# Encoder block on one core: head groups projected in order 0, 1, 2, the third rotated in a stack of its own, and its tiles stored by residue on the way out of PSUM

## The chip, the cores and the metric

The kernel runs on one core of a Trainium2 chip. The metric is the device time of one execution in microseconds (us). Five engines work side by side, each through its own queue in program order: TensorE (PE, matmuls; PEld is its weight load), VectorE (DVE), ScalarE (ACT), GpSimd (POOL) and SyncE (SP, which here issues most of the loads).

## The reference, cut to what matters

One layer over 512 positions of width 1024. Its attention branch has 12 heads of 128 dimensions in three groups of four, with dilations 1, 4 and 16, and a rotary turn of the first 32 dimensions of each query and key:

```python
q = partial_rope(q.reshape(B, S, n_heads, HEAD_DIM))
k = partial_rope(k.reshape(B, S, n_heads, HEAD_DIM))
for g, (window, dilation) in enumerate(ATTN_PATTERNS):        # (128,1), (512,4), (2048,16)
    sl = slice(g * HEADS_PER_GROUP, (g + 1) * HEADS_PER_GROUP)
    o_g, lse_g = dilated_window_attention(q[:, :, sl], k[:, :, sl], v[:, :, sl], dilation, window // (2 * dilation))
# partial_rope: concatenate([x1*cos - x2*sin, x2*cos + x1*sin, rest])
...
w_mix = jax.nn.softmax(jnp.stack(lses, axis=0), axis=0)
y_b = jnp.sum(w_mix[..., None] * o_all, axis=0).reshape(B, S, ATTN_GROUP_WIDTH)
```

Beside it stand a gated MLP branch (u, v through GELU, layer norm of v, a 128x128 spatial matmul), learned gates, an output projection and a feed-forward part of width 4096.

## The kernel before, in words

Everything is float32. A large matmul is done as three products of high and low parts (`mm3`, L84 to L86; a weight is split by ACT at L74 and DVE at L75, other tiles by ACT at L79 and DVE at L80). A projection of 128 features over 512 positions (`feature_tile`, PSUM tile `pf`) is 24 matmuls.

The attention stage runs over four values of `h`. `project_qk(h)` projects a query and a key tile for each of the three groups, six `pf` tiles in all, always with 128 features on the partitions and 512 positions along the row. Each tile is copied from PSUM by ACT twice: whole into `q1`, `k1` and so on (L331), and its first 32 rows into a stack `st` (L333), so that several tiles can be turned at once. `rotate` turns a stack: DVE swaps the halves of each 32 rows into `sw` (L311), POOL multiplies `sw` by the sine (L312), DVE multiplies `st` by the cosine (L313) and adds the two (L314), and ACT copies each 32 rows back into its tile (L316). Groups come in the order 1, 2, 0. Groups 1 and 2 share one stack (128 rows); group 0 has its own (64 rows).

Groups 1 and 2 work on positions by their residue modulo 4. The tiles keep natural order, and the score matmuls (`scores_b`, PSUM tile `psb`, L378, eight per value of `h`) pick every fourth column of query and key. Group 0 is split into high and low parts and scored in 128-position blocks (`scores_a`, tile `psa`). Each score tile goes through `softmax_tile` (DVE L364 and L366, ACT exponential L367). `mix(h)` weighs the groups: DVE prepares `xa`, PE multiplies it with a selection matrix (`pp`, L403), DVE and ACT work on four-column tiles up to `xc` (L405 to L424), PE does `pc` (L426), DVE gives `ca` (L430), and ACT scales the probabilities (L432, L434). `attend(h)` transposes the probabilities (`pt`, L453 and L466; split into `ptah`, `ptal`) and multiplies with the values (`py`, L483 to L490; L490 writes every fourth PSUM column). It runs within `project_qk(h + 1)`, and for the last `h` within the stage of the MLP branch.

After the attention loop comes the projection of v for the MLP branch (PSUM tile `pv`, 96 matmuls; GELU at L509 to L512, layer norm at L535 to L539 into `vln`), then four `pf` tiles for u, between which `pg` (L612) multiplies `vln` with the spatial weights. The weights of u are split by ACT (L74) and POOL (L75, input `uw`).

A scheduler puts the instructions of each engine's queue in an order when the kernel is built; the queues then run in that order and wait on semaphores. Pools give each named tile its buffers (`st` has two, `wpool` three weight tiles, PSUM tag `acc` four).

Of the kernel before, what the change touches and what calls it, by code (L numbers as in the profile page):

```python
# [10 lines left out]
F32 = mybir.dt.float32  # L11
F32R = mybir.dt.float32r
AF = mybir.ActivationFunctionType
ALU = mybir.AluOpType
PSUM = bass.MemoryType.PSUM

P = 128
S = 512
# [18 lines left out]
def block_kernel(ctx: ExitStack, tc: tile.TileContext, x, norm_mix_pre, w_in, b_gate, ln_v_gain, ln_v_bias,  # L37
                 w_spatial, b_spatial, w_branch_a, w_branch_b, w_out, norm_mix_post, norm_mlp_pre, w_up,
                 w_down, norm_mlp_post, ident_c, rope_c, mask_c, perm_c, out):
    nc = tc.nc  # L40
# [3 lines left out]
    def pool(stack, name, bufs=1, space=None, side=None):  # L44
        kw = {"side": side} if side else {}
        if space is not None:
            kw["space"] = space
        return stack.enter_context(tc.tile_pool(name=name, bufs=bufs, reuse_waits="tile", **kw))
# [14 lines left out]
    def wload(shape, srcs, name):  # L63
        raw = wpool.tile([P] + shape, F32, name=name, tag="raw")
        for dst, src in srcs(raw):
            nc.sync.dma_start(dst, src)
        return raw

    def wsplit(raw, pl=None, bufs=None, tag="w", sub=None):
        pl = pl or wpool  # L70
        shape = list(raw.shape)
        hi = pl.tile(shape, F32R, name="hi", tag=tag + "hi", bufs=bufs)
        lo = pl.tile(shape, F32R, name="lo", tag=tag + "lo", bufs=bufs)
        nc.scalar.activation(hi, raw, AF.Copy)  # L74
        (sub or nc.vector).tensor_tensor(lo, raw, hi.bitcast(F32), op=ALU.subtract)  # L75
        return hi, lo

    def split_into(hi, lo, src):
        nc.scalar.activation(hi, src, AF.Copy)  # L79
        return nc.vector.tensor_tensor(lo, src, hi.bitcast(F32), op=ALU.subtract)  # L80
# [199 lines left out]
    def feature_tile(wh, wl, nk, mh, ml, tag="acc"):  # L280
        ps = psA.tile([P, S], F32, name="pf", tag=tag, bufs={"acc": 4, "S": 2, "T": 1, "y": 1}[tag])
        for k in range(nk):
            mm3(ps, (wh[:, k], wl[:, k]), (mh[:, k], ml[:, k]), k == 0, k == nk - 1)
        return ps

    def fcols(wap, c0, nk, n, raw=None):
        return wap[:, c0:c0 + n].rearrange("(k p) c -> p k c", p=P)
# [3 lines left out]
    rows = gmlp.tile([32, P], F32, name="rows")  # L291
    wsp = gmlp.tile([P, 4, P], F32, name="wsp")
    proj = ExitStack()
    apool = pool(proj, "apool")
    rope = apool.tile([P, 2, S], F32, name="rope")
# [9 lines left out]
    by_r = perm[:, 2 * P:2 * P + 4].unsqueeze(1).unsqueeze(1)  # L305
    by_c = perm[:, 2 * P + 4:2 * P + 8].unsqueeze(1).unsqueeze(3)

    def rotate(st, tiles):
        rows = 32 * len(tiles)
        sw = apool.tile([P, S], F32, name="sw")  # L310
        nc.vector.stream_shuffle(sw[:rows], st[:rows], [(i + 16) % 32 for i in range(32)])  # L311
        nc.gpsimd.tensor_tensor(sw[:rows], sw[:rows], rope[:rows, 1], op=ALU.mult)  # L312
        nc.vector.tensor_tensor(st[:rows], st[:rows], rope[:rows, 0], op=ALU.mult)  # L313
        nc.vector.tensor_tensor(st[:rows], st[:rows], sw[:rows], op=ALU.add)  # L314
        for i, d in enumerate(tiles):
            nc.scalar.activation(d[0:32], st[32 * i:32 * i + 32], AF.Copy)  # L316

    def project_qk(h):
        got, tiles = {}, []
        for g in (1, 2, 0):  # L320
            if g == 2 and h:
                attend(h - 1)
            if g != 2:
                st, tiles = apool.tile([P, S], F32, name="st", bufs=2), []
            hd0 = (g * NH + h) * HD
            raw = wload([2, KD, P], lambda r: [(r[:, 0], fcols(w_in, COL_Q + hd0, KD, P)), (r[:, 1], fcols(w_in, COL_K + hd0, KD, P))], "qkw")
            for j, nm in enumerate("qk"):
                wh, wl = wsplit(raw[:, j])
                ps = feature_tile(wh, wl, KD, nhn, nln)
                d = apool.tile([P, S], F32, name=f"{nm}{g}")  # L330
                nc.scalar.activation(d, ps, AF.Copy)  # L331
                i = len(tiles)
                nc.scalar.activation(st[32 * i:32 * i + 32], ps[0:32], AF.Copy)  # L333
                tiles.append(d)
                got[nm, g] = d.rearrange("p (l r) -> p r l", r=4)
            if g == 2:
                rotate(st, tiles)
                scores_b(h, got)
            elif g == 0:
                rotate(st, tiles)  # L340
        for nm, t in zip("qk", tiles):
            w = S if nm == "q" else S + P
            o = 0 if nm == "q" else ROT
            hi = apool.tile([P, w], F32R, name=f"{nm}0h")
            lo = apool.tile([P, w], F32R, name=f"{nm}0l")
            split_into(hi[:, o:o + S], lo[:, o:o + S], t)
            if nm == "k":
                for z, y in ((hi, nc.scalar), (lo, nc.vector)):
                    zf = z.bitcast(F32)
                    for dst, src in ((z[:, 0:ROT], zf[:, S:S + ROT]), (z[:, S + ROT:], zf[:, ROT:2 * ROT])):  # L350
                        if y is nc.scalar:
                            y.activation(dst, src, AF.Copy)
                        else:
                            y.tensor_copy(dst, src)
            got[nm, 0] = (hi, lo)
        scores_a(h, got)

    stat = {}
    probs = {}
# [10 lines left out]
    def scores_b(h, got):  # L370
        md = small.tile([P, 2, 4], F32, name="mdb", bufs=2)
        stat[h, "md", "b"], stat[h, "m", "b"], stat[h, "d", "b"] = md, md[:, 0], md[:, 1]
        for r2 in range(2):
            ps = psA.tile([P, 2, 2, P], F32, name="psb", tag="S", bufs=2)
            for rr in range(2):
                r = 2 * r2 + rr
                for g in (1, 2):
                    nc.tensor.matmul(ps[:, rr, g - 1], got["q", g][:, r], got["k", g][:, r], start=True, stop=True)  # L378
            for rr in range(2):
                softmax_tile(h, "b", 2 * r2 + rr, ps[:, rr], masks[:, 4:6])  # L380

    def scores_a(h, got):
        md = small.tile([P, 2, 4], F32, name="mda", bufs=2)
        stat[h, "md", "a"], stat[h, "m", "a"], stat[h, "d", "a"] = md, md[:, 0], md[:, 1]
        (qh, ql), (kh, kl) = got["q", 0], got["k", 0]
        for c2 in range(2):
            ps = psA.tile([P, 2, 2, P], F32, name="psa", tag="S", bufs=2)
            for cc in range(2):
                c = 2 * c2 + cc
                qs, ks = slice(c * P, (c + 1) * P), slice(c * P, c * P + 2 * P)  # L390
                mm3(ps[:, cc], (qh[:, qs], ql[:, qs]), (kh[:, ks], kl[:, ks]), True, True)
            for cc in range(2):
                c = 2 * c2 + cc
                m = (masks[:, 0:3:2], masks[:, 1:3], masks[:, 1:3], masks[:, 1:4:2])[c]
                softmax_tile(h, "a", c, ps[:, cc], m)
# [40 lines left out]
    def attend(h):  # L436
        for _ in attend_steps(h):
            pass
# [55 lines left out]
    for h in range(NH):  # L494
        project_qk(h)
        mix(h)
# [96 lines left out]
    for g2 in range(2):  # L593
        raw = wload([KD, 2 * P], lambda r: [(r, fcols(w_in, COL_U + g2 * 2 * P, KD, 2 * P))], "uw")
        for j in range(2):
            g = 2 * g2 + j
            wh, wl = wsplit(raw[:, :, j * P:(j + 1) * P], sub=nc.gpsimd)
            ps = psA.tile([P, S], F32, name="pf", tag="acc" if g else "T", bufs=4 if g else 1)
# [87 lines left out]
    for d in range(GSTD):  # L686
        g2 = gate_rows(d - GSTD)
        raw = gate_raw(d)
        for br in range(2):
            ps = feature_tile(*wsplit(raw[:, :, 1 - br]), KD, nhn, nln)  # L690
# [85 lines left out]
    for t in range(4):  # L776
# [18 lines left out]
        r = rstd_of(ss, 1.0 / D)  # L795
# [187 lines left out]
def _constants():  # L983
    half = 16
    inv = (np.float32(500000.0) ** (-np.arange(0, 32, 2, dtype=np.float32) / np.float32(32))).astype(np.float32)
    ang = np.arange(S, dtype=np.float32)[:, None] * inv[None, :]
    cos, sin = np.cos(ang).astype(np.float32).T, np.sin(ang).astype(np.float32).T
    rope = np.tile(np.stack([np.concatenate([cos, cos]), np.concatenate([-sin, sin])]).astype(np.float32), (1, 4, 1))
    i = np.arange(P)[:, None]
    j = np.arange(P)[None, :]  # L990
    lo = i <= j
    hi = j <= i
    valid = [lo & (j >= ROT), lo, hi, hi & (j < ROT), np.abs(i - j) <= 64, (i - j) % 4 == 0]
    masks = np.stack([np.where(v, np.float32(0), np.float32(NEG)) for v in valid]).astype(np.float32)
    sel = (j // 4 == i % 32).astype(np.float32)
    by = [(np.arange(P)[:, None] % 4 == np.arange(4)[None, :]), (np.arange(P)[:, None] // 32 == np.arange(4)[None, :])]
    perm = np.concatenate([sel.T, sel] + [b.astype(np.float32) for b in by], axis=1).astype(np.float32)
    return {"ident_c": np.eye(P, dtype=np.float32), "rope_c": rope, "mask_c": masks, "perm_c": perm}
# [17 lines left out]
```

## Time and profile before

| what | value |
|---|---|
| median of 3 runs | 835.42 us (835.19 to 835.52) |
| the profiled execution | 831.64 us |
| its span, first to last instruction | 829.9 us |
| PE busy | 812.1 us (98%) |
| DVE, ACT, POOL busy | 489.7, 411.0, 58.0 us |
| mean granted TensorE clock | 0.995 |

A busy PE is a PE with a matmul in flight; it does not say at what pace. So beside the waits of PE one reads the distance between matmuls of a kind and the granted clock. Idle time of another engine matters only where PE waits for it.

### The profile page before, as it was taken

What the parts mean: (1) busy time and instruction counts of PE and PEld (TensorE: products, weight loads), DVE (VectorE), ACT (ScalarE), POOL (GpSimd) and SP (SyncE); (2) the same over time, 40 slices, a digit from 0 to 9 for tenths busy, and PEclk for the clock granted to TensorE, in tenths of its full rate; (3) what the DMA queues carried; (4) which work ended last, traced back from release to release, by engine and by line L of the source; (5) the groups of instructions that cost most, each with busy time, mean ns of one, the idle gap of its engine ahead of it and who ended that gap; (6) DMA issues with size and microseconds to landing.
All of it is one profiled execution on the core that took longest, in us unless ns stands there. A gap on an engine that the chain in (4) does not pass through costs nothing.

```text
span 829.9 us, 11578 instructions
## 1 busy us (share of the span) xinstructions
PE 812.1 (98%) x4629; PEld 721.4 (87%) x4629; DVE 489.7 (59%) x819; ACT 411.0 (50%) x689; POOL 58.0 (7%) x77
## 2 busy tenths in 40 slices
PE   9999999999999699999999999999999999999996
PEld 6899888888888488999998899999999888888885
DVE  6762245535353687787856559989888543333324
ACT  6342365857564535444535456666567533223311
POOL 3011010101012310000001210000000000000000
PEclk9999999999999899999999999999999999999999
DMA  9277323131312254342457221334333643222202
GB/s 311 98 256 209 86 72 102 51 102 51 102 52 57 58 199 127 94 115 77 129 177 226 104 102 52 112 117 129 103 102 103 228 152 102 90 82 87 98 1 102
DMA packets 84056, 95.73 MB, mean 115 GB/s; under 512 B 2417, under 2 KB 70033, under 8 KB 82978
## 3 DMA queue, kind: packets, MB, share of 16 engines
q1 hardware_dynamic: 80208, 77.60, 30.7%
q0 software_dynamic: 3792, 17.39, 6.1%
q8 instruction: 36, 0.59, 0.3%
q14 instruction: 18, 0.15, 0.1%
q10 hardware_dynamic: 2, 0.00, 0.0%
HBM read 86.60 MB, written 8.39 MB: 114 GB/s over the span
## 4 chain that ended last, share of the span: by engine, by line
PE 93%; DVE 4%; DMA 2%; ACT 1%; issue 0%; SPq 0%; DVEq 0%; POOLq 0%; ACTq 0%
PE pacc L885 11%; PE pd L84 9%; PE pd L86 9%; PE pd L85 9%; PE pf L84 8%; PE pf L85 8%; PE pf L86 8%; PE pgacc L560 6%; PE ptp L885 4%; PE pv L85 3%; PE pv L86 3%; PE pv L84 3%; PE pgS L560 2%; PE psb L378 2%; DMA w0raw<-in_w_in_dram 1%; PE py L490 1%
## 5 line engine op out<-in xcount | busy, mean ns | idle before, releaser
L84 PE MATMUL pf<-nh,hi 128*128 128x512 f32 x240 | 95.7, 399 | 0.3 <-DVE xd L428 0.3
L85 PE MATMUL pf<-nl,hi 128*128 128x512 f32 x240 | 95.2, 397 | 0.0
L86 PE MATMUL pf<-nh,lo 128*128 128x512 f32 x240 | 95.1, 396 | 0.0
L85 PE MATMUL pd<-hl,hh 128*128 128x512 f32 x224 | 87.2, 389 | 0.0
L84 PE MATMUL pd<-hl,hh 128*128 128x512 f32 x224 | 86.2, 389 | 0.0
L86 PE MATMUL pd<-hl 128*128 128x512 f32 x224 | 86.0, 389 | 0.0
L885 PE MATMUL pacc<-nt,hl 128*128 128x256 f32 x504 | 67.6, 280 | 0.1
L80 DVE TENSOR_TENSOR hl<-hid,hh 128x512 fp32r<-128x512 f32 x28 | 19.2, 692 | 75.6 <-ACT hh L79 75.6
L885 PEld LDWEIGHTS pacc<-nt,hl 128*128 128x128 f32 x504 | 62.6, 188 | 0.5 <-ACT hl L79 0.3
L75 DVE TENSOR_TENSOR lo<-qkw,hi 128x1024 fp32r<-128x1024 f32 x24 | 29.4, 1226 | 55.4 <-ACT hi L74 53.9
L79 ACT ACTIVATE hh<-hid 128x512 fp32r<-128x512 f32 x28 | 17.4, 630 | 89.0 <-PE pd L85 89.0
L84 PEld LDWEIGHTS pf<-nh,hi 128*128 128x128 f32 x240 | 45.7, 190 | 9.6 <-DVE xd L428 0.4
L86 PEld LDWEIGHTS pf<-nh,lo 128*128 128x128 f32 x240 | 45.6, 190 | 9.0
L85 PEld LDWEIGHTS pf<-nl,hi 128*128 128x128 f32 x240 | 45.6, 190 | 8.8
L86 PEld LDWEIGHTS pd<-hl 128*128 128x128 f32 x224 | 42.0, 188 | 8.8
L85 PEld LDWEIGHTS pd<-hl,hh 128*128 128x128 f32 x224 | 42.0, 188 | 8.8
L84 PEld LDWEIGHTS pd<-hl,hh 128*128 128x128 f32 x224 | 42.0, 188 | 8.5
L80 DVE TENSOR_TENSOR hl<-dnw,hl 128x1024 fp32r<-128x1024 f32 x32 | 39.1, 1225 | 13.9 <-ACT hl L79 13.9
L885 PE MATMUL pacc<-n,hl 128*128 128x256 f32 x336 | 45.2, 279 | 0.4 <-ACT z L910 0.4
L79 ACT ACTIVATE hl<-s 128x1024 fp32r<-128x1024 f32 x28 | 29.6, 1058 | 29.1 <-DVE s L869 10.8
L885 PEld LDWEIGHTS pacc<-n,hl 128*128 128x128 f32 x336 | 41.9, 188 | 0.6 <-ACT z L910 0.6
L74 ACT ACTIVATE hi<-qkw 128x1024 fp32r<-128x1024 f32 x24 | 25.4, 1058 | 32.1 <-PE pf L85 24.4
(315 smaller groups left out, 1966.9 us busy)
## 6 DMA issues: line engine op xcount, KB each, us to landing
upw<-in_w_up_dram SPq DMA_DIRECT2D x16, 1024.0 KB, 5.5
dnw<-in_w_down_dram SPq DMA_DIRECT2D x16, 1024.0 KB, 4.9
qkw<-in_w_in_dram SPq DMA_DIRECT2D x24, 512.0 KB, 5.4
gw<-in_w_in_dram SPq DMA_DIRECT2D x16, 512.0 KB, 5.1
slab<-in_w_in_dram SPq DMA_DIRECT2D x6, 1024.0 KB, 9.3
sum<-sum POOLq DMA_DIRECT2D x4, 1024.0 KB, 7.9
nt<-sum POOLq DMA_DIRECT2D x4, 1024.0 KB, 6.3
wow<-in_w_out_dram SPq DMA_DIRECT2D x4, 1024.0 KB, 4.9
```

The costliest lines, as they stand in the source:

```text
L74: nc.scalar.activation(hi, raw, AF.Copy)
L75: (sub or nc.vector).tensor_tensor(lo, raw, hi.bitcast(F32), op=ALU.subtract)
L79: nc.scalar.activation(hi, src, AF.Copy)
L80: return nc.vector.tensor_tensor(lo, src, hi.bitcast(F32), op=ALU.subtract)
L84: nc.tensor.matmul(ps, ah, bh, start=start, stop=False)
L85: nc.tensor.matmul(ps, ah, bl, start=False, stop=False)
L86: return nc.tensor.matmul(ps, al, bh, start=False, stop=stop)
L378: nc.tensor.matmul(ps[:, rr, g - 1], got["q", g][:, r], got["k", g][:, r], start=True, stop=True)
L490: nc.tensor.matmul(o, v12[:, g, r, hs], ptb[r // 2][:, r % 2, g], start=False, stop=(r == 3 and g == 1), skip_group_check=True)
L560: nc.tensor.matmul(ps, a[:, j], b[:, j], start=first and not (j or i), stop=(j == KH - 1 and i == 2), skip_group_check=True)
L885: nc.tensor.matmul(ps, a[:, j], b[:, j], start=first and not (j or m), stop=(j == KH - 1 and m == 2), skip_group_check=True)
```

## The change: what it does

The groups are projected in the order 0, 1, 2. Groups 0 and 1 share the stack of 128 rows; group 2 gets rows 64 to 127 of another. `scores_a` follows the first rotation, `scores_b` comes last. For groups 1 and 2 the two copies from PSUM read every fourth column, so that the tiles lie in SBUF by residue, and the score matmuls read 128 columns in a row. The rotary table has natural order for its first 64 rows and residue order for the other 64. The product with the sine is done by DVE.

```diff
-    def rotate(st, tiles):
-        rows = 32 * len(tiles)
+    def rotate(st, tiles, r0):
+        rows = slice(r0, r0 + 32 * len(tiles))
         sw = apool.tile([P, S], F32, name="sw")
-        nc.vector.stream_shuffle(sw[:rows], st[:rows], [(i + 16) % 32 for i in range(32)])
-        nc.gpsimd.tensor_tensor(sw[:rows], sw[:rows], rope[:rows, 1], op=ALU.mult)
-        nc.vector.tensor_tensor(st[:rows], st[:rows], rope[:rows, 0], op=ALU.mult)
-        nc.vector.tensor_tensor(st[:rows], st[:rows], sw[:rows], op=ALU.add)
+        nc.vector.stream_shuffle(sw[rows], st[rows], [(i + 16) % 32 for i in range(32)])
+        nc.vector.tensor_tensor(st[rows], st[rows], rope[rows, 0], op=ALU.mult)
+        nc.vector.tensor_tensor(sw[rows], sw[rows], rope[rows, 1], op=ALU.mult)
+        nc.vector.tensor_tensor(st[rows], st[rows], sw[rows], op=ALU.add)
         for i, d in enumerate(tiles):
-            nc.scalar.activation(d[0:32], st[32 * i:32 * i + 32], AF.Copy)
+            nc.scalar.activation(d[0:32], st[r0 + 32 * i:r0 + 32 * i + 32], AF.Copy)
     def project_qk(h):
-        got, tiles = {}, []
-        for g in (1, 2, 0):
-            if g == 2 and h:
-                attend(h - 1)
-            if g != 2:
-                st, tiles = apool.tile([P, S], F32, name="st", bufs=2), []
+        got, tiles, r0 = {}, [], 0
+        st = apool.tile([P, S], F32, name="st", bufs=2)
+        for g in range(3):
+            if g == 2:
+                st, tiles, r0 = apool.tile([P, S], F32, name="st", bufs=2), [], 64
+                if h:
+                    attend(h - 1)
...
-                nc.scalar.activation(d, ps, AF.Copy)
-                i = len(tiles)
-                nc.scalar.activation(st[32 * i:32 * i + 32], ps[0:32], AF.Copy)
+                view = ps.rearrange("p (l r) -> p r l", r=4) if g else ps
+                i = r0 + 32 * len(tiles)
+                for dst, src in ((st[i:i + 32], view[0:32]), (d, view)):
+                    nc.scalar.activation(dst.rearrange("p (r l) -> p r l", r=4) if g else dst, src, AF.Copy)
                 tiles.append(d)
-                got[nm, g] = d.rearrange("p (l r) -> p r l", r=4)
-            if g == 2:
-                rotate(st, tiles)
-                scores_b(h, got)
-            elif g == 0:
-                rotate(st, tiles)
+                got[nm, g] = d.rearrange("p (r l) -> p r l", r=4)
+            if g:
+                rotate(st, tiles, r0)
+            if g == 1:
+                scores_a(h, split_qk(tiles[:2]))
+        scores_b(h, got)
+
+    def split_qk(tiles):        # the split of q0, k0 that stood at the end of project_qk
...
-    rope = np.tile(np.stack([np.concatenate([cos, cos]), np.concatenate([-sin, sin])]).astype(np.float32), (1, 4, 1))
+    rope = np.stack([np.concatenate([cos, cos]), np.concatenate([-sin, sin])]).astype(np.float32)
+    by_residue = rope.reshape(2, 32, S // 4, 4).transpose(0, 1, 3, 2).reshape(2, 32, S)
+    rope = np.concatenate([rope, rope, by_residue, by_residue], axis=1)
```

The queues change as follows at three places. Lines of the changed kernel are up to seven higher (L378 becomes L383, L426 becomes L431, L539 becomes L544).

First, PE at the end of the attention loop, behind the last products of the values with the probabilities of h = 2 (`py`). Before:

```order
L86 MATMUL pv<-hi,nl 128x512
L490 MATMUL py<-ptb,v_89 128x128 x4
L403 MATMUL pp<-xa,perm 128x32
L426 MATMUL pc<-xc,perm 128x16
L84 MATMUL pf<-nh,hi 128x512
```

PE in the changed kernel at the same place:

```order
L85 MATMUL pv<-lo,nh 128x512
L495 MATMUL py<-ptb,v_89 128x128 x4
L408 MATMUL pp<-xa,perm 128x32
L86 MATMUL pv<-hi,nl 128x512
...
L86 MATMUL pv<-hi,nl 128x512
L431 MATMUL pc<-xc,perm 128x16
L84 MATMUL pv<-hi,nh 128x512
```

All 96 `pv` matmuls stood ahead of `pp` and `pc` before; now 34 of them stand between the two and 27 behind `pc`. For h = 1 and h = 2 the distance from `pp` to `pc` grows from 34 `pf` matmuls to 43.

Second, DVE at the last rotation of h = 3. Before, that of group 0, with its split behind it:

```order
L311 STREAM_SHUFFLE sw<-st 64x512
L313 TENSOR_TENSOR st<-st,rope 64x512
L314 TENSOR_TENSOR st<-st,sw 64x512
L80 TENSOR_TENSOR ptal<-pt,ptah 128x512
L80 TENSOR_TENSOR q0l<-q_2067,q0h 128x512
L80 TENSOR_TENSOR k0l<-k_2099,k0h 128x512
```

DVE in the changed kernel at the last rotation of h = 3, that of group 2:

```order
L311 STREAM_SHUFFLE sw<-st 64x512
L312 TENSOR_TENSOR st<-st,rope 64x512
L313 TENSOR_TENSOR sw<-sw,rope 64x512
L369 ISA p,mda<-psa,masks 128x256
L369 ISA mda 128x1
L369 ISA p,mda<-psa,masks 128x256
L369 ISA mda 128x1
L314 TENSOR_TENSOR st<-st,sw 64x512
```

The sum of the rotation now stands behind two softmax steps of group 0, which wait for `psa` on PE. On PE, 14 projection matmuls, `psa`, four transposes, six `py` and 15 projection matmuls stand between the end of the last key tile and the first `psb`.

Third, DVE in the layer norm of v, behind the end of the `pv` matmuls. Before:

```order
L519 COPY cols<-ptr 128x32
L539 TENSOR_SCALAR vln<-vln,mv,rs_out 128x512
L512 SCALAR_TENSOR_TENSOR vln<-gt,pv 128x512
L80 TENSOR_TENSOR ptal<-pt,ptah 128x512
L512 SCALAR_TENSOR_TENSOR vln<-gt,pv 128x512
L535 BN_STATS st_2360<-vln 128x6
L80 TENSOR_TENSOR ptal<-pt,ptah 128x512
```

DVE in the changed kernel at the same place:

```order
L542 BN_AGGR mv<-st_2332 128x2
L80 TENSOR_TENSOR ptal<-pt,ptah 128x512
L540 BN_STATS st_2346<-vln 128x6
L90 TENSOR_SCALAR rs_in<-mv 128x1
L80 TENSOR_TENSOR ptal<-pt,ptah 128x512
L515 SCALAR_TENSOR_TENSOR gt<-gt,pv 128x512 x2
L542 BN_AGGR mv<-st_2346 128x2
L544 TENSOR_SCALAR vln<-vln,mv,rs_out 128x512
```

The two `ptal` of the last `attend` moved ahead of the first `vln` normalization. On PE the first two `pg` of u's first tile follow the last `attend`'s first products, the third stands 18 `pf` and eight `py` matmuls further on. Behind the start of the gates only a few neighbours on PE change places, and SP issues the same loads in the same sequence throughout.

More of the change, by code (lines that the diff above doesn't have):

```diff
@@ L330, in project_qk @@
                 d = apool.tile([P, S], F32, name=f"{nm}{g}")
-                nc.scalar.activation(d, ps, AF.Copy)
-                i = len(tiles)
-                nc.scalar.activation(st[32 * i:32 * i + 32], ps[0:32], AF.Copy)
+                view = ps.rearrange("p (l r) -> p r l", r=4) if g else ps
+                i = r0 + 32 * len(tiles)
+                for dst, src in ((st[i:i + 32], view[0:32]), (d, view)):
+                    nc.scalar.activation(dst.rearrange("p (r l) -> p r l", r=4) if g else dst, src, AF.Copy)
                 tiles.append(d)
-                got[nm, g] = d.rearrange("p (l r) -> p r l", r=4)
-            if g == 2:
-                rotate(st, tiles)
-                scores_b(h, got)
-            elif g == 0:
-                rotate(st, tiles)
+                got[nm, g] = d.rearrange("p (r l) -> p r l", r=4)
[5 more added lines that the diff above has]
+    def split_qk(tiles):
+        got = {}
         for nm, t in zip("qk", tiles):
@@ L355, in project_qk @@
             got[nm, 0] = (hi, lo)
-        scores_a(h, got)
+        return got
     stat = {}
```

## The prediction

> **What bounds the kernel now.** I read the page first (busy time, the chain that ended last), then the waits of PE alone, then the attention stage by groups, the chain in order of time, and the clock around the longest wait.
>
> ```profile
> PE 812.1 (98%) x4629; PEld 721.4 (87%) x4629; DVE 489.7 (59%) x819; ACT 411.0 (50%) x689; POOL 58.0 (7%) x77
> PE 93%; DVE 4%; DMA 2%; ACT 1%; issue 0%; SPq 0%; DVEq 0%; POOLq 0%; ACTq 0%
> PE pc L426 <- DVE xc L424: 4.7, 1, 4.7
> PE pt L466 <- DVE ptal L80: 2.6, 1, 2.6
> PE pf L84 <- DVE xd L428: 0.3, 1, 0.3
> PE py L483 <- ACT ptah L79: 0.3, 1, 0.3
> ```
>
> PE is the bound: 93% of the chain lies on it. So only two things can move the time: fewer or faster matmuls, and the waits of PE. The waits are few, and the largest stand where the attention loop ends. The last four rows are PE's waits: total, times, longest.
>
> Next, the pace of the score matmuls, beside matmuls of the same 128x128 shape whose operands lie in a row:
>
> ```profile
> L378 PE MATMUL psb<-k,q 128*128 128x128 f32 x64 | 16.7, 416 | 0.0
> L490 PE MATMUL py<-ptb,v 128*128 128x128 f32 x64 | 8.6, 275 | 0.0
> L378 PEld LDWEIGHTS psb<-k,q 128*128 128x128 f32 x64 | 15.7, 326 | 0.2
> L490 PEld LDWEIGHTS py<-ptb,v 128*128 128x128 f32 x64 | 8.1, 191 | 0.2
> ...
> 114.24 0.93 PE psb L378 x4
> 115.41 2.79 PE psb L378 x12
> 118.43 0.23 PE pf L85
> 153.05 3.73 PE psb L378 x16
> 181.53 0.89 PE py L490 x8
> 195.41 0.93 PE psb L378 x4
> 196.57 0.92 PE psb L378 x4
> 238.77 0.93 PE psb L378 x4
> 239.93 0.92 PE psb L378 x4
> ```
>
> The last rows are the chain: start, length, what. Each `psb` takes 0.233 us of PE (3.73/16), each `py` 0.111 (0.89/8), each `pf` or `pv` 0.23.
>
> **The change, part by part.**
>
> *Scores from tiles stored by residue (gain 7.8).* Both operands of `psb` are now read with a step of four columns; afterwards both lie in a row, as those of `py` do. Their number stays: 64 in the trace. 64 x (0.233 - 0.111) = 7.8 us, all on PE and so on the path. Ends: 0, if the step does not set the pace, and 7.8; I take 7.8, because the weight load too is 326 ns against 191 for the same shape.
>
> *Copies out of PSUM with a step (ACT; 0 on the path).*
>
> ```profile
> L331 ACT ACTIVATE k<-pf 128x512 f32<-128x512 f32 x11 | 6.4, 581 | 0.1
> L316 ACT ACTIVATE k<-st 32x512 f32<-32x512 f32 x12 | 7.6, 630 | 0.3
> 95.00:130.00 35.00, 35.00 (x155) 29.66 (x154) 13.45 (x30) 18.95 (x35) 3.44 (x2) 1.00 0.30 83
> 170.00:200.00 30.00, 30.00 (x156) 26.22 (x155) 11.97 (x43) 16.79 (x35) 1.73 (x1) 1.00 0.27 80
> 230.00:260.00 30.00, 30.00 (x151) 25.91 (x151) 16.56 (x55) 19.92 (x43) 5.88 (x3) 1.00 0.24 71
> ```
>
> (The windows give PE, PEld, DVE, ACT, POOL busy time, then the clock.) Eight copies per h take the step. No row has ACT reading PSUM that way. The floor is no extra; the nearest row is the stepped weight load, 326 - 191 = 135 ns more for 128 columns, so 0.54 us for 512. Eight of them are 4.3 us per h; ACT is busy some 60% of these windows, so it keeps about 16 us free in the 41 us of one h. I take the upper end, 0.54, and cost it at nothing on the path where the next part shows cover for it. The Trainium skill ("Advanced Engine Details and Errata", PSUM Cachelines) says that any non-contiguous access to PSUM significantly slows matmuls. Row L490 disagrees for writes: it writes every fourth column and keeps 0.111. Reads by ACT no run here shows; by the rule they would be dearer, which is the first rival below.
>
> *The last rotation of each h (group 2, 64 rows; 0).*
>
> ```profile
> L311 DVE STREAM_SHUFFLE sw<-st 64x512 f32<-64x512 f32 x4 | 2.9, 731 | 0.0
> L313 DVE TENSOR_TENSOR st<-st,rope 64x512 f32<-64x512 f32 x4 | 2.7, 681 | 0.1
> L312 POOL TENSOR_TENSOR sw<-sw,rope 64x512 f32<-64x512 f32 x4 | 7.0, 1752 | 53.3 <-DVE sw L311 29.2 <-DVE nm L366 24.1
> L364 DVE CUSTOM_DVE_ANT_0 p<-psa,masks 128x256 f32<-128x256 f32 x8 | 3.1, 418 | 0.0
> ```
>
> The sine product costs DVE eight more products of 0.68 (5.5 us in all) instead of 1.75 each on POOL; a rotation alone is no longer for it (0.73 + 3 x 0.68 = 2.8 us). Behind the end of the last key tile PE has 14 `pf` (3.2), `psa` (12 at about 0.12, 1.4), four transposes and six `py` (1.2) and 15 `pf` (3.4): `psb` is due after 9.2 us. The chain: the sum of the rotation queues behind two softmax steps, and these wait for half of `psa` (3.2 + 0.7), 0.4 each: 4.7; sum 0.7: 5.4; the `ptb` copy and two copies of 0.63 on ACT: 7.2. Two us are spare. The stepped copies delay the start of the rotation by 0.54, which hides, since the sum waits for `psa` anyway. Without this cover each h would pay what exceeds 2 us. The 128-row rotation has 62 `pf` (14 us) between its last tile and `psa`. POOL loses 14 us of work which nobody on the path waited for.
>
> *The wait of `pc` (gain 6.9).*
>
> ```profile
> 272.71 2.04 DVE L409 TENSOR_TENSOR big<-mab,mdb 128x4 f32<-128x4 f32 x1
> 276.64 0.17 DVE L424 TENSOR_TENSOR xc<-cf,perm 128x16 f32<-128x16 f32 x1
> 277.00:280.00 3.00, 2.73 (x7) 2.19 (x8) 1.41 (x4) 3.00 (x8) 0.00 (x0) 0.50 0.08 25
> 278.34 0.63 PE L85 MATMUL pf<-nl,hi 128*128 128x512 f32 x1
> 278.76 0.63 PE L86 MATMUL pf<-nh,lo 128*128 128x512 f32 x1
> 281.32 0.58 PE L86 MATMUL pf<-nh,lo 128*128 128x512 f32 x1
> 272.39 2.34 POOL L75 TENSOR_TENSOR lo<-uw,hi 128x1024 fp32r<-128x1024 f32 x1 [4.47 <-ACT hi L74]
> ```
>
> PE waits 4.7 us for the DVE chain, then 0.3, and then runs at a granted clock of 0.50: eight `pf` stand 0.42 apart (278.34 to 278.76) in place of 0.23, 1.5 us, and `pc` itself some 0.4. Sum 6.9. Afterwards 34 `pv` (7.8 us) lie between `pp` and `pc`. From `pp` to `xc` DVE took under 5 us, 2 of them beside a POOL product. But now group 2's scores come last, so the chain also runs from `psb`: the queue puts the exponentials of group 0, a weight split on ACT and DVE, two pairs of softmax steps and four exponentials ahead, which I add up to about 9 us; `pc` is due 12 us after `psb` starts. Spare about 3, and one POOL product of 2.3 can eat most of it. So gain 6.9 at best, 0 if all the slack is misjudged; I take 6.9. Next late is what follows `pv`.
>
> *The layer norm of v (gain 3.0, loss 3.5).*
>
> ```profile
> 278.93 1.28 DVE L510 SCALAR_TENSOR_TENSOR gt<-gt,pv 128x512 f32<-128x512 f32 x2 [1.04 <-ACT gt L509]
> 286.55 2.46 DVE L539 TENSOR_SCALAR vln<-vln,mv,rs_out 128x512 f32<-128x512 f32 x1
> 298.77 0.55 DVE L539 TENSOR_SCALAR vln<-vln,mv,rs_out 128x512 f32<-128x512 f32 x1 [0.44 <-POOL rs_out L96]
> ```
>
> The 2.6 and 0.3 us that PE waits for `ptal` and `ptah` should go, as the two `ptal` now precede the slow normalization: 2.9, say 3.0. But in the kernel before, the stretch from the first GELU product to the last `vln` lasts 298.77 + 0.55 - 278.93 = 20.4 us, and it began 8 us after the last `pv`, because `pc` held it. Now it begins at once, while PE gets to the `pg` that needs the last `vln` after 8 transposes, 24 `pf`, about 4 us of small matmuls, 21 `pf` and eight `py`: 0.9 + 5.5 + 4 + 4.8 + 0.9 = 16.1 us. DVE needs 20.4, less a 0.7 product that moved behind, less up to 1.9 by which the 2.46 exceeds its 0.55 sister. So PE waits 1.7 to 4.9 here, in several pieces. I take 3.5.
>
> *The rest (0).* The loads keep their sequence and sizes on SP; weights of a tile are split two tiles ahead.
>
> Sum: 7.8 + 6.9 + 3.0 - 3.5 = 14.2 us. The profiled execution would go from 831.64 to 817.4. It stands 3.8 us below the median of the runs shown; carried over in us, 835.42 - 14.2 = 821.2.
>
> **The rivals.**
>
> 1. *The stepped copies make ACT the bound (slower).* If ACT's read of PSUM costs far more than the weight load suggests, the eight copies fill ACT. Its 16 us free per h are used up at 2.0 us extra per copy; beyond that each h grows by eight times the rest. At 16/8 + 14.2/32 = 2.4 us extra (3.0 in place of 0.58) the gain is gone; at 3 us extra it is 4 x 8 = 32 us lost, 853. The Trainium skill's rule ("Advanced Engine Details and Errata", PSUM Cachelines), taken at its worst, leads here; it gives no size. For it: no row shows such a read. Against it: the step costs PE a factor of two, not five.
>
> 2. *The wait of `pc` stays.* The exponentials of both groups, the weight split and a POOL product then end after the 34 `pv`. The stall, once some 4 us long, brings the half clock with it: the 6.9 are not gained, 828. For it: 3 us of slack against one 2.3 us POOL product. Against it: the three inner h have 43 matmuls there and no POOL product.
>
> 3. *The MLP part takes more.* If DVE's burst is held by POOL's splits of u again, and the half clock follows the wait, the loss is 4.9 + 1.9 rather than 3.5: 824.5.
>
> 4. *The step does not set the pace of `psb`.* Then the 7.8 fall away: 829. Against it stand both rows of L378.
>
> **How the numbers follow.** Forecast as summed, 817 to 823.5: 0.60. Rival 3, to 827: 0.17. Rival 2: 0.09. Rival 4: 0.04. More than I count, under 817: 0.03. A mixture of losses that ends within 0.2%: 0.02. Rival 1: 0.05. The likeliest gives 821.2; the range 816 to 827 takes in rival 3 and the bounds of the layer norm, and leaves out rivals 1, 2 and 4 and the mixture, 0.20 together. So faster by over 0.2% 0.93, within 0.2% (1.7 us, about what a measurement can tell from no change) 0.02, slower 0.05.
>
> **What would show it.** `psb` matmuls 0.11 us apart and weight loads near 190 ns; no wait of PE for `xc`, and no granted clock near 0.5 beside it; waits of PE for `vln` or for ACT ahead of `pg`, 2 to 5 us together; stepped copies between 0.58 and 1.1 us; no POOL product in the attention stage. The prediction is wrong if PE waits in the attention loop itself, for `q2` or `k2`, or if `psb` keeps its pace.

## The result: 20 us faster, and the profile after

The changed kernel takes 815.28 us (814.79 to 815.90, 4 runs) beside 835.31 us (834.69 to 835.52): ratio 0.976, interval 0.9745 to 0.9779. The direction was forecast; the time lies 5.9 us below the 821.2 and 0.7 us below the range. Its four runs stand in two pairs, at 814.79 and at 815.8 to 815.9; the profiled one, with a span of 813.0 us, is of the faster pair.

Page of the changed kernel, then PE's longest waits (total, times, longest):

```profile
PE 801.5 (99%) x4629; PEld 711.2 (87%) x4629; DVE 493.4 (61%) x827; ACT 413.2 (51%) x689; POOL 43.7 (5%) x69
PE 93%; DVE 3%; DMA 1%; ACT 1%; issue 0%; DVEq 0%; POOLq 0%; POOL 0%; ACTq 0%
```

```profile
PE idle L153 <- DVE onesq L59: 1.1, 1, 1.1
PE prs L530 <- ACT wst L528: 0.7, 1, 0.7
PE pt L180 <- DVE xn L176: 0.6, 1, 0.6
PE pd L84 <- DVE gs L592: 0.5, 1, 0.5
```

The waits for `xc`, `xd`, `ptal` and `ptah` (7.9 us) are gone. Two new ones stand in their place: 0.7 us for `wst`, and 0.5 us for `gs`, much later, at 422 us. The rows for `onesq` and `xn` belong to the start of the kernel and were there before.

Score matmuls and stepped copies of the changed kernel, by groups (80 to 300 us of the span):

```profile
L383 PE MATMUL psb<-k,q 128*128 128x128 f32 x64 | 8.3, 275 | 0.0
L383 PEld LDWEIGHTS psb<-k,q 128*128 128x128 f32 x64 | 8.0, 192 | 0.3
L335 ACT ACTIVATE k<-pf 128x512 f32<-128x512 f32 x12 | 7.2, 600 | 0.2
L335 ACT ACTIVATE st<-pf 32x512 f32<-32x512 f32 x24 | 14.0, 584 | 0.5
```

`psb` and its weight load have the durations of `py` (275 and 191 ns): 64 of them now take 64 x 0.111 = 7.1 us. The copies, two thirds of them stepped, average 0.58 to 0.60 us, as before (0.58): ACT reads every fourth PSUM column at next to no extra.

The stretch where `pc` stood, by windows (PE, PEld, DVE, ACT, POOL busy, then the granted clock):

```profile
250.00:255.00 5.00, 5.00 (x26) 4.21 (x26) 2.35 (x13) 2.75 (x9) 0.31 (x1) 1.00 0.49 125
255.00:260.00 5.00, 5.00 (x25) 4.16 (x24) 0.34 (x2) 2.36 (x6) 2.76 (x3) 1.00 0.18 56
```

PE is busy throughout and the clock stays at 1.00.

### The profile page after: what moved, and what is told of

Read it like the earlier page. It is cut to its first block, busy times and chain, and to the rows that moved or that the text cites. A ratio compares the mean times of both kernels' runs of the same rounds, so it can differ in the third digit from the quotient of the medians.

```text
span 813.0 us, 11561 instructions
## 1 busy us (share of the span) xinstructions
PE 801.5 (99%) x4629; PEld 711.2 (87%) x4629; DVE 493.4 (61%) x827; ACT 413.2 (51%) x689; POOL 43.7 (5%) x69
## 4 chain that ended last, share of the span: by engine, by line
PE 93%; DVE 3%; DMA 1%; ACT 1%; issue 0%; DVEq 0%; POOLq 0%; POOL 0%; ACTq 0%
PE pacc L890 11%; PE pd L84 9%; PE pd L85 9%; PE pd L86 9%; PE pf L85 9%; PE pf L84 9%; PE pf L86 9%; PE pgacc L565 6%; PE ptp L890 4%; PE pv L85 3%; PE pv L86 3%; PE pv L84 3%; PE pgS L565 2%; PE psb L383 1%; PE py L495 1%; DMA upw<-in_w_up_dram 1%
## 5 line engine op out<-in xcount | busy, mean ns | idle before, releaser
L79 ACT ACTIVATE hl<-dnw 128x1024 fp32r<-128x1024 f32 x32 | 33.4, 1048 | 12.4 <-PE pacc L890 7.5
```

## The experiments

The two profiled executions lie 16.9 us apart, the medians 20.0. The first theory to test: the rest is half clock that typical executions of the kernel before pay, and its first profiled execution did not.

**The kernel before, again.** No edit.

> The kernel before, unchanged, profiled once more, to see whether the 831.64 us of its first profiled execution is typical. The two profiled executions differ by 16.9 us, the medians by 20.0. Theory (clock): the first profiled execution was one in which TensorE came back to full clock early behind the wait of pc; this profile should show 834 to 836 us, a longer stretch at a granted clock near 0.5 behind pc (8 to 9 us instead of 4.3), and the same 4.7 us wait. Rival (elsewhere): the 3 to 4 us lie in another stage or are spread over the span, and the stretch behind pc is the same 4.3 us. Ratio to before 1.000.

Its 12 runs took 830.75 to 836.45 us, median 834.20; the profiled one 835.56, span 833.8. PE's two longest waits, then the windows behind them:

```profile
PE pc L426 <- DVE xc L424: 4.7, 1, 4.7
PE pt L466 <- DVE ptal L80: 2.6, 1, 2.6
```

```profile
276.50:277.50 1.00, 0.56 (x2) 0.50 (x2) 0.37 (x3) 0.71 (x2) 0.00 (x0) 0.71 0.59 156
277.00:280.00 3.00, 2.73 (x7) 2.24 (x8) 1.34 (x4) 3.00 (x8) 0.00 (x0) 0.50 0.09 27
280.00:283.00 3.00, 3.00 (x8) 2.32 (x8) 1.69 (x4) 2.77 (x7) 0.00 (x0) 0.50 0.00 0
283.00:286.00 3.00, 3.00 (x13) 2.33 (x13) 2.61 (x8) 0.52 (x1) 0.45 (x1) 0.88 0.00 0
289.00:292.00 3.00, 0.67 (x4) 0.70 (x5) 3.00 (x5) 1.35 (x3) 1.40 (x2) 0.76 0.00 0
292.00:295.00 3.00, 3.00 (x10) 2.17 (x10) 3.00 (x5) 0.60 (x1) 0.00 (x0) 0.50 0.00 0
295.00:300.00 5.00, 5.00 (x19) 3.88 (x18) 4.56 (x15) 0.63 (x1) 1.39 (x3) 0.76 0.00 0
```

Two windows of the first profiled execution of the same kernel:

```profile
274.50:275.50 1.00, 0.00 (x0) 0.00 (x0) 0.99 (x4) 0.00 (x0) 0.92 (x3) 0.70 0.00 0
290.00:295.00 5.00, 4.64 (x25) 3.75 (x26) 5.00 (x10) 1.47 (x3) 0.00 (x0) 1.00 0.00 0
```

The waits are the same to 0.1 us, but the half clock is not. It lasts until 283.7 here (0.88 over the three us from 283), against 281.7 in the first execution, and a second stretch follows the wait for `ptal`, where the first execution had a clock of 1.00. The expected place was right; that a second stretch exists was not expected, and the one behind `pc` lasts 6.8 us rather than 8 to 9. By start times the first stretch costs 1.0 us more than in the first execution and the second 2.9: together the 3.9 by which the spans differ.

The first stretch is equally long in both. In the first execution the mean of 0.70 puts the drop at about 274.9, two us before `pc`, while PE was idle; here 0.71 puts it at 276.9, as work began. What a wait costs thus hangs on where the drop falls, and that differs from run to run. The Trainium skill ("TensorE: Matmul & The Clock Gate", What's actually happening) gives windows of 3.4 us that run on their own, whatever the kernel does; the stretches (274.9 to 281.7 and 276.9 to 283.7, 6.8 us each) agree with two of them.

**The step alone.** The kernel before, order 1, 2, 0 and POOL's product kept, tiles by residue. The rotary table is stored by residue too, so the two products of group 0's rotation read it with a step:

```diff
...
-                nc.scalar.activation(d, ps, AF.Copy)
+                view = ps.rearrange("p (l r) -> p r l", r=4) if g else ps
...
-                got[nm, g] = d.rearrange("p (l r) -> p r l", r=4)
+                got[nm, g] = d.rearrange("p (r l) -> p r l", r=4)
...
```

> The kernel before with one part of the change: the tiles of groups 1 and 2 are stored by residue, order 1, 2, 0, the stacks and the sine product on POOL stay. Theory: psb goes to 0.111 us each, 7.8 to 8.2 us faster, about 827.3; the wait of pc (4 to 5 us) and the half clock behind it stay; the stepped copies take 0.58 to 0.60 us. Rival (the step does not set the pace): no change, 835. Rival (stepped copies load ACT): PE waits for ACT and less than 5 us are gained.

825.68 us (823.75 to 828.12), ratio 0.990 (0.9877 to 0.9922): 8.3 us faster than the 834.01 beside it. The row of `psb`, then PE's waits:

```profile
L383 PE MATMUL psb<-k,q x64: 271/275/356, 114.1 to 234.8; 128*128 128x128 f32 x64
```

```profile
PE pc L431 <- DVE xc L429: 4.7, 1, 4.7
PE pt L471 <- DVE ptal L80: 2.6, 1, 2.6
```

The term of the step is confirmed, and the wide spread of the kernel before stays with its waits.

**The order alone.** The changed kernel with tiles, and the rotary table, in natural order; `psb` reads every fourth column again:

```diff
...
-                view = ps.rearrange("p (l r) -> p r l", r=4) if g else ps
+                view = ps
...
-                got[nm, g] = d.rearrange("p (r l) -> p r l", r=4)
+                got[nm, g] = d.rearrange("p (l r) -> p r l", r=4)
...
```

> The changed kernel without the storing by residue: groups in order 0, 1, 2, the third in its own stack, sine on VectorE, tiles in natural order and psb reading every fourth column. Theory (clock): the wait of pc goes, and with it all of the half clock: 12 us faster, about 823.3, of which 9.2 are seen in the profiles. Rival (the rest is elsewhere): only the 9.2 us that the two profiles show, about 826. psb stays at 0.233 us.

822.91 us (822.80 to 823.03), ratio 0.9869 (0.9849 to 0.9888): 11.1 us faster. Its `psb` matmuls:

```profile
L383 PE MATMUL psb<-k,q x64: 398/415/492, 125.0 to 256.1; 128*128 128x128 f32 x64
```

It has no wait for `xc` or `ptal`, and its four runs lie within 0.23 us of each other. 11.1 is nearer to the 12 of the clock theory than to the 9.2. With the step's 8.3 it adds up to 19.4: the two parts account for nearly the whole gain.

**A filled wait in the kernel before.**

```diff
-        nc.tensor.matmul(pp, perm[:, 0:P], xa, start=True, stop=True)
+        pin = nc.tensor.matmul(pp, perm[:, 0:P], xa, start=True, stop=True)
+        if h == NH - 1:
+            fill = psA.tile([P, S], F32, name="fill", tag="S", bufs=2)
+            for _ in range(20):
+                with tc.issue_after(pin.ins):
+                    pin = nc.tensor.matmul(fill, nh[:, 0, 0:P], nhn[:, 0], start=True, stop=True)
```

> The kernel before with 20 extra matmuls of 0.23 us (4.6 us; their results are not used) between pp and pc of the last h, so that PE does not idle while VectorE works on xc. The wait is then filled but not shortened. Theory (clock): only the half clock behind pc goes. The first profiled execution shows 1.9 us of that; if typical executions lose 3 to 4 us more there, the kernel gets 5 to 6 us faster, about 830. Rival (the rest is elsewhere): 2 us or less, 833.5.

828.93 us (828.10 to 829.98), ratio 0.9943 (0.9926 to 0.996): 5.1 us faster with 20 more matmuls. But the scheduler also moved the last `attend`, and the later wait shrank (the wait, then a window behind the filled one):

```profile
PE pt L471 <- DVE rs_in L90: 0.9, 1, 0.9
```

```profile
278.00:283.00 5.00, 5.00 (x26) 4.13 (x25) 3.39 (x6) 4.76 (x11) 0.00 (x0) 1.00 0.00 0
```

So about 2 of the 5.1 us are shorter waits (2.6 and 0.3 us for `ptal` and `ptah` before, 0.9 now). The direction speaks for the clock; the size isn't clean. In the next pair the queues of PE differ by the extra matmuls alone.

**The wait put back, and filled.** The changed kernel, with the last 60 `pv` matmuls held behind `pc`; in the second, 12 extra matmuls stand in the wait.

```diff
+                        with tc.issue_after(after.ins) if after and count >= 12 else nullcontext():
+                            mm3(accs[r], ...)
...
-    token_major(COL_V, ..., evac_v)
+    token_major(COL_V, ..., evac_v, after=held[-1])      # held[-1] is pc of the last h
```

> The changed kernel, unchanged, beside the next three on one chip. Every theory: 815 us, a spread of about 1 us over its runs (the kernel before spreads over 5), ratio 0.976 to 0.979.

> The changed kernel with its last 60 pv matmuls held behind pc, so that pp and pc of the last h stand one pv apart and PE waits for VectorE's chain again; nothing else moves. By the profile of the changed kernel the chain ends 2.7 us after that pv. Theory (clock): the wait costs itself plus a stretch at half clock, 2.7 + 2 to 4 = 4.7 to 6.7 us, about 820.5, and the runs spread more widely. Rival (a wait costs only its length): 2.7 us, 818.

> As the kernel with the last 60 pv held behind pc, with 12 extra matmuls (2.8 us, their results are not used) filling the wait. Theory (clock): only the length of the wait is lost, about 818, with a small spread and no half clock. Rival (a wait costs only its length): the same as without the extra matmuls, within 0.5 us.

On one chip: changed kernel 814.80 (814.68 to 815.78), wait put back 819.85 (819.32 to 821.34), wait filled 817.61 (817.53 to 818.57); ratios to the kernel before 0.9768 (0.9747 to 0.9788), 0.9828 (0.9806 to 0.985), 0.9801 (0.9781 to 0.9822). The wait put back, its windows, and the windows of the filled one:

```profile
PE pc L436 <- DVE xc L434: 2.6, 1, 2.6
```

```profile
251.00:253.00 2.00, 0.00 (x0) 0.00 (x0) 1.62 (x10) 0.21 (x1) 0.00 (x0) 0.98 0.41 97
253.00:256.30 3.30, 3.19 (x9) 2.62 (x10) 0.39 (x3) 3.29 (x8) 0.00 (x0) 0.50 0.00 0
256.30:260.00 3.70, 3.70 (x18) 3.07 (x17) 0.00 (x0) 1.07 (x2) 1.00 (x1) 1.00 0.01 4
```

```profile
251.00:253.00 2.00, 2.00 (x10) 1.67 (x9) 1.59 (x10) 0.23 (x2) 0.00 (x0) 1.00 0.53 125
253.00:256.30 3.30, 3.30 (x16) 2.55 (x16) 0.62 (x5) 3.07 (x8) 0.00 (x0) 1.00 0.02 5
```

In 253.0 to 256.3 the waiting kernel does 9 matmuls, the filled one 16. With the wait the median rises by 5.05 us; with 2.8 us of unused matmuls in its place it rises by 2.8. How much of the 2.2 between them is the clock? The profiled executions, with spans of 818.1 and 816.8, lie 1.3 us apart, and 1.2 of it has arisen by the end of the half clock: the `pv` matmul that starts at 256.26 in the waiting kernel starts at 255.02 in the filled one. So 1.2 us is shown to be the clock, more than the 0.5 that the rival allowed. Both executions fall behind the profiled one of the changed kernel by another 1.0 us between 515 and 630 us, and the filled one, at 818.57, is the slowest of its four, a us above the others. The rest of the 2.2 may be no more than that; why some executions lose this us isn't known.

**The sine product alone,** back on POOL in the changed kernel, and on VectorE in the kernel before (one line each in `rotate`).

> The changed kernel with the sine product back on POOL (1.75 us in place of 0.68, eight times). Theory: the rotation has two us of cover, the product on POOL runs beside the cosine product on VectorE and makes the rotation some 0.5 us longer, so nothing: 814.8 to 815.3. Rival (VectorE's product is what took the rotation off the path): PE waits for q2 and k2, 2 us or more lost, 817.

> The kernel before with the sine product on VectorE and nothing else. pp and pc stay next to each other in PE's queue. Theory: no gain beyond 1 us either way, 834 to 836, as the rotation was hidden; the wait of pc and the half clock stay. Rival: the product was part of the gain, 2 us or more faster.

On POOL in the changed kernel: 814.82 us (814.58 to 815.00), ratio 0.9765 (0.9747 to 0.9783). No difference, as expected. On VectorE in the kernel before: 829.76 (829.01 to 830.79) beside 834.70, ratio 0.9947 (0.9929 to 0.9965). That is 4.9 us faster where under 1 was expected; the theory was wrong here. Its wait, the step of the chain that took 2.04 us before, and POOL beside it:

```profile
PE pc L426 <- DVE xc L424: 2.9, 1, 2.9
```

```profile
273.81 0.15 DVE L409 TENSOR_TENSOR big<-mab,mdb 128x4 f32<-128x4 f32 x1
270.92 2.35 POOL L75 TENSOR_TENSOR lo<-uw,hi 128x1024 fp32r<-128x1024 f32 x1 [4.30 <-ACT hi L74]
```

POOL's split of u now ends at 273.27, before `big`; in the kernel before it ended at 274.73 (272.39 + 2.34), and `big`, begun at 272.71, at 274.75. So a 0.15 us product on VectorE was held to the end of a POOL product. The Trainium skill ("SBUF — State Buffer", SBUF: two separate sides) has this as an exclusive lock of the port pair the two engines share, and these rows agree. In the changed kernel the place of the product made no difference, so the likely cause is the order: the scheduler set POOL and the layer norm in another one, whose waits are shorter. The wait for `ptal` is gone, and the only half clock in this stage lasts from 276.4 to 279.8. So the 4.9 is not a third part of the gain; it removes some of the same waits, and of the clock behind them, as the change of order does.

**The new wait for `wst`.** The changed kernel with the transposes of the spatial weights issued within u's first tile rather than behind it:

```diff
+                if g == 0 and k == 5:
+                    with tc.issue_after(ins.ins):
+                        spatial_weights()
...
-            if g == 0:
-                with tc.issue_after(ins.ins):
-                    spatial_weights()
```

> The changed kernel with the transposes of the spatial weights issued before the end of u's first tile, so that ACT copies wst ahead of the second ptb. Theory: the one wait that the changed kernel has in this stage (0.7 us, prs for wst) goes: 0.5 to 0.7 us faster, 814.6. Rival: DVE's burst takes its place as PE gets to pg earlier, no change.

813.88 us (813.74 to 814.01), ratio 0.9754 (0.9734 to 0.9774), 0.9 us under the changed kernel's 814.80 on the same chip, with no overlap of their runs. The row for `prs` is gone from PE's waits. This version is the fastest of all.

## Why the prediction was right, and where it fell short

- **The step (7.8).** Right: 8.3 us alone, and `psb` at 275 ns with weight loads at 192. Rival 4 is refuted.
- **The stepped copies (0 on the path).** Right, and even the taken 0.54 us extra was far too much: about 0.02. Rival 1 needed 2.4. The PSUM rule of the Trainium skill ("Advanced Engine Details and Errata", PSUM Cachelines) speaks of matmuls; the prediction carried it over to ACT's reads, and these rows don't bear that out.
- **The last rotation (0).** Right: no wait of PE for `q2` or `k2`, with the sine on either engine.
- **The wait of `pc` (6.9).** The mechanism was right and the size was not: this is the larger of the two terms that failed. 1.9 of it was half clock, read from one execution in which a part of the slow stretch fell into the idle time and the wait for `ptal` drew no stretch at all. In the execution profiled again that clock cost 1.9 + 3.9 = 5.8 us. The working saw that this execution stood 3.8 us under the median and carried the difference over as a constant; it was part of what the change removes.
- **The layer norm of v (gain 3.0, loss 3.5).** The gain came. The loss was mis-sized, the second term that failed: 0.7 in place of 3.5, and it is ACT's `wst`, not the last `vln`. The timeline's rows of VectorE's burst and of the `pg` matmul that needs its end, in the changed kernel, then VectorE's stretch as a window, before and in the changed kernel:

```profile
263.25 1.37 DVE L515 SCALAR_TENSOR_TENSOR gt<-gt,pv 128x512 f32<-128x512 f32 x2 [4.45 <-ACT gt L514]
271.90 2.75 DVE L544 TENSOR_SCALAR vln<-vln,mv,rs_out 128x512 f32<-128x512 f32 x1
279.98 0.99 DVE L544 TENSOR_SCALAR vln<-vln,mv,rs_out 128x512 f32<-128x512 f32 x2
264.47 1.03 PE L458 MATMUL pt<-ident,p 128*128 128x128 f32 x8
282.12 0.38 PE L617 MATMUL pg<-wst,vln 128*128 128x128 f32 x2
278.93:299.32 20.39, 17.41 (x90) 14.06 (x89) 17.73 (x36) 10.27 (x19) 5.53 (x7) 0.93 0.00 0
263.25:280.97 17.72, 17.03 (x99) 14.21 (x98) 17.44 (x36) 9.87 (x17) 8.28 (x9) 1.00 0.26 67
```

VectorE took 280.97 - 263.25 = 17.7 us and began 1.2 us before PE's last `pv` group was done. That is the low end of what was worked out, but by luck: the slow normalization did not go (2.75 us), and VectorE is as busy as before. What went is its idle time within the stretch, 20.39 - 17.73 = 2.7 us before and 0.3 now, which the prediction had counted as work. PE took 17.6 us where the sum said 16.1: 0.7 is the wait for `wst`, and the eight `py` are 16 matmuls in the trace, 1.7 us rather than 0.9. Rival 3 is refuted by the same rows.

By terms: step 8.2 (15.3 us of `psb` in the chain before, 7.1 after), waits 7.9, half clock 5.8, new waits -0.7 and -0.5: 20.7, against 20.8 between the spans of the kernel before as profiled again and the changed kernel. The forecast had 14.2 by taking 1.9 for the clock and 3.5 for the loss. With 5.8 and 0.7 in their places it would have been 20.9. The list of rivals held losses almost alone: for more gain than was counted it left 0.03.

Why did the same 2.6 us wait for `ptal` lower the clock in one profiled execution of the kernel before and not in the other? Within each profiled execution the clock changes only at whole multiples of 3.41 us from its other changes: profiled again, it drops at 276.9 and 290.6 and returns at 283.7 and 297.4. Stretches cut by that spacing, of the first execution (two), of the second, and of the kernel with the wait put back (PE's busy time is the second figure):

```profile
285.13:288.54 3.41, 2.25 (x15) 1.52 (x13) 2.51 (x6) 3.32 (x6) 2.73 (x2) 1.00 0.01 2
288.54:291.96 3.42, 1.60 (x11) 1.40 (x12) 3.42 (x7) 1.44 (x3) 0.88 (x2) 1.00 0.00 0
287.15:290.57 3.42, 1.20 (x7) 0.72 (x6) 3.15 (x4) 2.60 (x6) 3.04 (x2) 1.00 0.01 2
249.49:252.90 3.41, 1.00 (x8) 0.69 (x7) 2.19 (x13) 1.53 (x6) 0.00 (x0) 1.00 0.76 197
```

In the first execution the wait is split over two stretches, which hold 1.2 and 1.8 us of idle time, and the clock stays. In the second, 2.2 us fall into one stretch, and the clock drops at its end; with the wait put back 2.4 us do the same. In all profiled executions, from 100 to 330 us, the six stretches at full clock with 2.2 us or more of idle PE are followed by half clock and those with up to 1.3 are not; of two with 1.8 one is (the step alone) and one is not. So the phase decides what a wait of this length costs. This is read from seven drops; what stays open is the exact limit, and no run set the phase.

## What to carry to other kernels

Where PE is the bound, read the pace of small matmuls beside others of their shape: here operands read with a step of four columns cost a factor of two (0.233 against 0.111 us), and a copy out of PSUM that had to happen anyway put them in a row for 0.02 us. Price a wait of PE at its length plus the half clock behind it, and take that from several executions: here a wide spread of the runs went with such waits. Before trusting the gain of one edit, look at how it moved the other queues: changing one product's engine brought 4.9 us here, most likely by the order alone.

## What the runs showed of the hardware

- A PE wait of 2.6 us was enough to bring the granted clock to 0.50 for 3.4 us of work (wait put back); 20 or 12 matmuls of no use in a wait kept it at 1.00. A wait of the same length that fell across two stretches of 3.41 us left it at 1.00 (the first execution of the kernel before).
- Kernels without the long waits vary little (0.23 us over four runs with the order alone, 1.1 for the changed kernel), the kernel before by 5.7 us over 12. Its runs at a mean granted clock of 0.995 took 830.8 and 831.5 us, those at 0.989 took 835.2 to 835.6.
- ACT reads every fourth column of PSUM at the same duration as columns in a row: 0.60 against 0.58 us for 512.
